# In-projection of a hybrid encoder layer: raw weight blocks fetched one and a half blocks ahead instead of one

## The chip, the cores and the metric

The kernel runs on one core of a Trainium2 chip. Its metric is the device time of one execution in microseconds; lower is better. Instructions are issued on five engines, each of which runs its own stream in order: PE (TensorE), DVE (VectorE), ACT (ScalarE), POOL (GpSimd) and SP (SyncE, which here only issues transfers). ACT issues transfers too, from the same stream as its arithmetic.

## The reference

One layer of a bidirectional encoder, sequence length 1024, model width 1024, float32 in and out. Everything starts with one wide projection whose columns are shared out to three branches and three gates:

```python
xn = rmsnorm(x, norm1_w[l])
p = xn @ w_in[l]
z, xbc, dt_raw, p_rwkv, p_hgrn, p_gate = jnp.split(p, in_splits, axis=-1)
y_ssm  = ssd_branch(z, xbc, dt_raw, ...) @ w_branch_ssm[l]
y_rwkv = rwkv7_branch(p_rwkv, ...)       @ w_branch_rwkv[l]
y_hgrn = hgrn2_branch(p_hgrn, ...)       @ w_branch_hgrn[l]
gates = jax.nn.sigmoid(p_gate).reshape(b, L, N_BRANCH, D_MODEL)
mixed = gates[:, :, 0] * y_ssm + gates[:, :, 1] * y_rwkv + gates[:, :, 2] * y_hgrn
x = x + mixed @ w_out[l]
h_gate, h_up = jnp.split(rmsnorm(x, norm2_w[l]) @ ffn_w_in[l], 2, axis=-1)
x = x + (jax.nn.silu(h_gate) * h_up) @ ffn_w_down[l]
```

The part of the RWKV branch that this document meets often is its preparation: tanh and sigmoid of the low-rank inputs, the decays `exp(-0.6065 * sigmoid(...))`, and the normalised key `kk = k*k_k * rsqrt(sum(...))`, which the kernel computes as an Exp of a Ln.

## The kernel before, in words

**Blocks of the in-projection.** The columns of `w_in` are cut into blocks of 128 (one of 32). One block is a *job* in the class `Jobs`. Job i needs its weights as two fp32r tiles, `wh` (the rounded weights) and `wl` (what the rounding left). `load_w` makes them: a DMA of 512 KB brings the raw block into a tile `wr` (L219, on ACT's queue from the fifth job on), ACT casts it to `wh` (L221), and POOL or DVE subtracts to get `wl` (L223). All three have two buffers. A job then runs 48 matmuls, 24 for each half of the sequence (L330, L331, L332, eight k-tiles of three), and ACT copies each half out of PSUM (L408 or L272).

**When weights are asked for.** `Jobs.steps(i)` is a generator: at its start it calls `load(i + 1)`, so that the raw DMA, the cast and the subtraction of the next block stand one whole block ahead in the order in which the code is written. One step is one k-tile.

**Work between the steps.** The branches call `J.fill(n)` to put n steps between their own instructions, `J.need(job)` to finish a certain job. In the RWKV preparation (`rwkv`, loop over p = 0 to 3, each p a pair of heads) the numbers come from the table `FILL["r1"]`. For p = 0 the written order is: tanh of `wad` (L459), job 2 to its end, sigmoid of its result (L464), sigmoids into `av` (L578) with 3 steps, two rounds of sigmoids into `sg` (L586) and a scan, with 3 steps behind each, then `explog(g)` (L591), then squares, Ln into `kk` (L603), Exp of `kk` (L604), and, in `decays`, Exps into `E` (L622) and `Em` (L623).

**What sets the final order.** The program is built with a scheduler that reorders each engine's stream by a simulated timeline; the written order is a priority, not the result. ACT evaluates functions from sets of tables, of which one is active; ACT_TABLE_LOAD makes another active. Where the scheduler has put the instructions, a later pass walks through ACT's stream and puts a load before each function that the active set lacks. The kernel places one load of its own per p, in `explog`, which activates a set that holds Exp and Ln together:

```python
def explog(g):
    ins = g.nc.scalar.preload_act_table_set("natural_log_exp_and_others")
    g.tc.keep_in_program_order(ins)
```

`keep_in_program_order` pins the load behind the one ACT instruction that was written immediately before it, and behind nothing else. The load has no operands, so the scheduler may put it anywhere after that instruction.

**Further names.** `vx`, `kx`, `rx` are token-shifted projections, `AR` and `BK` the products of `kk`, `rx`, `kx` with the decays, `vps` the transposes of `vx` (PE, L674), `Aps` small Gram products of `AR` and `BK` (PE, L653), `A_sb` their masked copy (DVE, L654), which goes out to DRAM as `As` and comes back as `At` for a triangular inverse on DVE (`lanes`, L483 and L485).

Of the kernel before, what the change touches and what calls it, by code (L numbers as in the profile page):

```python
# [9 lines left out]
F32 = mybir.dt.float32  # L10
# [8 lines left out]
P = 128  # L19
# [3 lines left out]
KT = D // P  # L23
# [25 lines left out]
def f32(ap):  # L49
    return ap.bitcast(F32)  # L50
# [131 lines left out]
class Split:  # L182


    def __init__(self):
        self.hi, self.lo = ([], []), ([], [])
# [25 lines left out]
        x.add(half, hi, lo)  # L212


def load_w(g, src, kt, n=P, tag="w"):

    nc = g.nc
    raw = g.wpool.tile([P, KT, P], F32, tag=tag + "r", name=tag + "r", bufs=g.wraw_bufs)
    g.wq.dma_start(raw[:, :kt, :n], src.rearrange("(k p) c -> p k c", p=P))  # L219
    hi = g.wpool.tile([P, KT, P], F32R, tag=tag + "h", name=tag + "h", bufs=2)  # L220
    nc.scalar.copy(hi[:, :kt, :n], raw[:, :kt, :n])  # L221
    lo = g.wpool.tile([P, KT, P], F32R, tag=tag + "l", name=tag + "l", bufs=2)
    g.lo_eng.tensor_sub(lo[:, :kt, :n], raw[:, :kt, :n], f32(hi[:, :kt, :n]))  # L223
    return hi, lo
# [11 lines left out]
def proj(g, c0, cb, n=P, wsrc=None, x=None, kt=KT):  # L236

    src = (g.A["w_in"][0] if wsrc is None else wsrc)[:, c0:c0 + n]
    whi, wlo = load_w(g, src, kt, n)
    for half in range(2):  # L240
        ps = g.mmps.tile([P, 512], F32, tag="mm", name="mm")
        mm3(g, ps[:n, :], whi, wlo, x or g.x, kt, half, n)
        cb(half, ps[:n, :])


class Jobs:
# [2 lines left out]

    def __init__(self, g):  # L250
        self.g, self.jobs, self.it, self.w = g, [], None, None
        self.started = self.taken = 0

    def add(self, c0, begin, half, end, n=P):
# [22 lines left out]
    def get(self, buf, t):  # L277
        self.need(buf.jobs[t])
        return buf.ap[t]

    def load(self, i):
        g, job = self.g, self.jobs[i]
        g.wq = g.nc.sync if i < 4 else g.nc.scalar
        if i < 4:
            g.lo_eng = g.nc.vector if i < 3 else g.nc.gpsimd
        return load_w(g, g.A["w_in"][0][:, job.c0:job.c0 + job.n], KT, job.n)

    def first(self, half):

# [30 lines left out]
    def steps(self, i):  # L320
        g, job = self.g, self.jobs[i]
        w = self.w or self.load(i)
        self.w = self.load(i + 1) if i + 1 < len(self.jobs) else None
        job.begin()
        n, x = job.n, g.x
        for half in range(2):
            ps = g.mmps.tile([P, 512], F32, tag="mm", name="mm")
            for k in range(KT):
                xh, xl = x.hi[half][k], x.lo[half][k]
                g.nc.tensor.matmul(ps[:n], w[0][:, k, :n], xh, start=(k == 0), stop=False)  # L330
                g.nc.tensor.matmul(ps[:n], w[0][:, k, :n], xl, start=False, stop=False)  # L331
                g.nc.tensor.matmul(ps[:n], w[1][:, k, :n], xh, start=False, stop=(k == KT - 1))  # L332
                if k == KT - 1:
                    job.half(half, ps[:n])
                    if half == 1:
                        job.end()
                        job.done = True
                yield
# [1640 lines left out]
def start(es, tc, A):  # L1979
# [37 lines left out]
    def trans(half):  # L2017
        with tc.tile_pool(name="n1ps", bufs=4, space=PSUM) as pp:
            transpose_split(g, x, half, xs[half * 4:half * 4 + 4], g.vec["norm1_w"], new, pp)

    g.x_load, g.x_rows, g.x_trans = load, rows, trans
    load(0)
    setup_consts(g, tp)
    n1w = vector_rows(g, tp, "n", [[("norm1_w", A["norm1_w"].rearrange("o (k p) -> (o k) p", p=P), 8)]], nc.scalar)
# [111 lines left out]
```

## Time and profile before

| what | value |
|---|---|
| median of 3 runs | 2424.53 us (2424.19 to 2427.28) |
| the profiled execution's own time | 2423.01 us |
| its span in the trace | 2421.3 us |
| mean granted TensorE clock | 0.973 of full speed |
| PE busy | 2272.7 us (94%) |
| DVE busy | 1570.6 us (65%) |
| ACT busy | 988.7 us (41%) |
| POOL busy | 1040.8 us (43%) |
| DMA | 306.23 MB, mean 126 GB/s |
| chain that ended last | PE 61%, DVE 20%, POOL 5%, DMA 5%, issue 4%, ACT 4% |

The busy time is what an engine's own instructions took; its complement is waiting. The chain is followed back from the last instruction: at each step to whatever released it, or to the instruction before it on its engine, so its shares say which engine the time was spent on along the one path that ended last. The profiled execution is 1.5 us (0.06%) under the median of the runs, and 1.7 us of its time lies outside the span.

### The profile page before, as it was taken

How to read it: one execution, taken by the hardware profiler on the slowest of the kernel's cores; microseconds unless marked ns; L12 is line 12 of the kernel's file. 1: busy time of each engine (PE TensorE's matmuls, PEld its weight loads, DVE VectorE, ACT ScalarE, POOL GpSimd, SP SyncE). 2: the span in 40 equal slices, each digit the busy share in tenths (PEclk: the TensorE clock that was granted, in tenths of full speed). 3: DMA queues.
4: the chain of work that ended last, by engine and by line, in shares of the span. 5: the costliest groups of instructions: out<-in, count | busy, mean ns of one | idle time of the engine just before them, and what ended most of it. 6: DMA issues, size and time to landing. Idle time of an engine off the chain costs nothing.

```text
span 2421.3 us, 37438 instructions
## 1 busy us (share of the span) xinstructions
PE 2272.7 (94%) x14785; PEld 1838.1 (76%) x14785; DVE 1570.6 (65%) x2041; ACT 988.7 (41%) x1436; POOL 1040.8 (43%) x817
## 2 busy tenths in 40 slices
PE   8998999999998998998999889999899999999895
PEld 6776778788777877887678567888688888877674
DVE  5678764455558568545856776442764554479999
ACT  6554532222466655435134154332433333344333
POOL 4433331543134335202941841430454444457985
PEclk9999999999999999999999999999999999999998
DMA  5455784764442232245545555541232222244211
GB/s 151 122 139 136 176 212 112 225 199 124 142 150 98 82 118 79 75 160 146 135 156 142 129 191 193 168 130 61 66 101 87 79 87 79 98 163 131 95 54 70
DMA packets 381212, 306.23 MB, mean 126 GB/s; under 512 B 111273, under 2 KB 323149, under 8 KB 381037
## 3 DMA queue, kind: packets, MB, share of 16 engines
q1 hardware_dynamic: 260909, 225.71, 31.7%
q10 hardware_dynamic: 119936, 77.61, 11.1%
q8 instruction: 116, 1.90, 0.3%
q0 software_dynamic: 192, 0.52, 0.1%
q14 instruction: 59, 0.48, 0.1%
HBM read 209.68 MB, written 94.11 MB: 125 GB/s over the span
## 4 chain that ended last, share of the span: by engine, by line
PE 61%; DVE 20%; POOL 5%; DMA 5%; issue 4%; ACT 4%; SPq 1%; ACTq 0%; DVEq 0%; POOLq 0%
PE mm L330 7%; PE mm L331 7%; PE mm L332 7%; PE ps L1588 6%; PE ps L1589 6%; PE ps L1590 6%; DVE ab L1805 3%; DVE acc L1927 2%; PE mm L231 2%; PE mm L232 2%; PE mm L233 2%; DMA E<-cumd 2%; POOL E L1369 2%; DVE rb L1805 1%; PE mm L1588 1%
## 5 line engine op out<-in xcount | busy, mean ns | idle before, releaser
L330 PE MATMUL mm<-x,wh 128*128 128x512 f32 (+1 forms) x1232 | 500.3, 406 | 0.6 <-ACT wh L221 0.5
L331 PE MATMUL mm<-x,wh 128*128 128x512 f32 (+1 forms) x1232 | 492.6, 400 | 0.0
L332 PE MATMUL mm<-x,wl 128*128 128x512 f32 (+1 forms) x1232 | 489.9, 398 | 0.0
L330 PEld LDWEIGHTS mm<-x,wh 128*128 128x128 f32 (+1 forms) x1232 | 232.8, 189 | 62.0 <-issue 10.3
L332 PEld LDWEIGHTS mm<-x,wl 128*128 128x128 f32 (+1 forms) x1232 | 232.8, 189 | 54.2 <-issue 4.6
L331 PEld LDWEIGHTS mm<-x,wh 128*128 128x128 f32 (+1 forms) x1232 | 232.8, 189 | 53.7 <-issue 7.0
L1589 PE MATMUL ps<-xb,rb 128*128 128x512 f32 x432 | 168.3, 390 | 0.0
L1590 PE MATMUL ps<-xb,rb 128*128 128x512 f32 x432 | 168.3, 390 | 0.0
L1588 PE MATMUL ps<-xb,rb 128*128 128x512 f32 x432 | 168.3, 390 | 0.0
L221 ACT CAST wh<-wr 128x1024 fp32r<-128x1024 f32 (+2 forms) x103 | 100.2, 973 | 109.4 <-PE mm L331 87.4
L1588 PE MATMUL ps<-rb,ab 128*128 128x512 f32 x308 | 125.9, 409 | 18.3 <-DVE acc L1927 17.4
L223 POOL TENSOR_TENSOR wl<-wr,wh 128x1024 fp32r<-128x1024 f32 x30 | 79.2, 2640 | 133.9 <-ACT wh L221 109.9
L1589 PE MATMUL ps<-rb,ab 128*128 128x512 f32 x308 | 123.7, 402 | 2.9 <-POOL rb L1805 2.9
L223 DVE TENSOR_TENSOR wl<-wr,wh 128x1024 fp32r<-128x1024 f32 (+2 forms) x73 | 95.2, 1303 | 44.9 <-ACT wh L221 44.8
L1590 PE MATMUL ps<-rb,ab 128*128 128x512 f32 x308 | 122.4, 400 | 1.5 <-DVE ab L1805 1.5
L1752 ACT CAST rb<-fs 128x512 fp32r<-128x512 f32 x85 | 52.6, 622 | 167.2 <-PE ps L1590 117.7
L272 ACT COPY st<-mm 128x512 f32<-128x512 f32 x130 | 75.3, 580 | 99.1 <-PE mm L332 82.9
L1369 POOL TENSOR_TENSOR E<-E,cums 128x1024 f32<-128x1024 f32 x32 | 69.3, 2178 | 65.5 <-DMA E<-cumd 45.3
L810 DVE TENSOR_TENSOR Gc<-Gps,mk 128x256 f32<-128x256 f32 x64 | 27.2, 425 | 106.0 <-PE Gps L807 59.9
L231 PE MATMUL mm<-oh,wh 128*128 128x512 f32 x224 | 89.5, 403 | 6.5 <-DVE gt L1492 4.3
L1927 DVE TENSOR_TENSOR acc<-acc,ps 128x512 f32<-128x512 f32 x148 | 94.1, 674 | 0.0
L1589 PEld LDWEIGHTS ps<-xb,rb 128*128 128x128 f32 x432 | 81.1, 188 | 16.9
(504 smaller groups left out, 5397.2 us busy)
## 6 DMA issues: line engine op xcount, KB each, us to landing
wr<-in_w_in_dram ACTq DMA_DIRECT2D x74, 512.0 KB
fr<-in_ffn_w_in_dram SPq DMA_DIRECT2D x44, 512.0 KB
E<-cumd SPq DMA_DIRECT2D x32, 512.0 KB
pg<-st ACTq DMA_DIRECT2D x48, 256.0 KB
gt<-pg SPq DMA_DIRECT2D x24, 512.0 KB
ad<-a SPq DMA_DIRECT2D x22, 512.0 KB
dr<-in_ffn_w_down_dram SPq DMA_DIRECT2D x22, 512.0 KB
ar<-ad SPq DMA_DIRECT2D x22, 512.0 KB
```

Source lines behind the costliest of these rows:

```text
L221: nc.scalar.copy(hi[:, :kt, :n], raw[:, :kt, :n])
L223: g.lo_eng.tensor_sub(lo[:, :kt, :n], raw[:, :kt, :n], f32(hi[:, :kt, :n]))
L231: nc.tensor.matmul(ps, whi[:, k, :n], xh, start=(k == 0), stop=False)
L330: g.nc.tensor.matmul(ps[:n], w[0][:, k, :n], xh, start=(k == 0), stop=False)
L331: g.nc.tensor.matmul(ps[:n], w[0][:, k, :n], xl, start=False, stop=False)
L332: g.nc.tensor.matmul(ps[:n], w[1][:, k, :n], xh, start=False, stop=(k == KT - 1))
L1369: nc.gpsimd.tensor_tensor(e, e, cs.unsqueeze(2).broadcast_to([P, 8, P]), SUB)
L1588: nc.tensor.matmul(ps, ah, bh, start=(i == 0), stop=False)
L1589: nc.tensor.matmul(ps, ah, bl, start=False, stop=False)
L1590: nc.tensor.matmul(ps, al, bh, start=False, stop=(i == n - 1))
L1805: eng.tensor_sub(blk[:, 1], s, f32(blk[:, 0]))
L1927: nc.vector.tensor_add(m[j], m[j], ps)
```

## The change

`load_w` is split: `load_raw` issues the DMA of the raw block alone, and `load_w` takes a raw tile that is already there. A new method `fetch(i)` calls `load_raw` for job i and keeps the tile; `steps(i)` calls `fetch(i + 2)` at the start of its second half, for jobs from the fifth on. The cast and the subtraction stay where they were. Buffer counts are the same.

```diff
+def load_raw(g, src, kt, n=P, tag="w"):
     raw = g.wpool.tile([P, KT, P], F32, tag=tag + "r", name=tag + "r", bufs=g.wraw_bufs)
     g.wq.dma_start(raw[:, :kt, :n], src.rearrange("(k p) c -> p k c", p=P))
+    return raw
+
+def load_w(g, src, kt, n=P, tag="w", raw=None):
+    nc = g.nc
+    if raw is None:
+        raw = load_raw(g, src, kt, n, tag)
     hi = g.wpool.tile([P, KT, P], F32R, tag=tag + "h", name=tag + "h", bufs=2)
...
+    def source(self, i):
+        job = self.jobs[i]
+        return self.g.A["w_in"][0][:, job.c0:job.c0 + job.n], KT, job.n
+
+    def fetch(self, i):
+        if 4 <= i < len(self.jobs) and i not in self.raws:
+            self.g.wq = self.g.nc.scalar
+            self.raws[i] = load_raw(self.g, *self.source(i))
+
     def load(self, i):
...
-        return load_w(g, g.A["w_in"][0][:, job.c0:job.c0 + job.n], KT, job.n)
+        return load_w(g, *self.source(i), raw=self.raws.pop(i, None))
...
         for half in range(2):
+            if half == 1:
+                self.fetch(i + 2)
             ps = g.mmps.tile([P, 512], F32, tag="mm", name="mm")
```

**What it does to the built program.** On PE, DVE, POOL and SP the instruction streams of the two programs are the same from end to end: the same operations in the same order with the same semaphores, wait values and memory addresses. On ACT all instructions but the table loads are the same and in the same order, the raw DMAs and the casts among them. Only the table loads differ: 52 before, 58 now. Lines shift: L219 is now L217, L221 is L227, L376 is L395, and from L408 on a line of before is 19 lower in the new file (L459 is L478, L603 is L622, L604 is L623, L622 is L641, L623 is L642).

ACT's stream at the tanh of the preparation, before (`av` is the shifted low-rank input, `wr` a raw weight block, `wah` the rounded tanh):

```order
L413 ACTIVATE av<-pt,mu_c_451 128x1024
L219 DMA wr<-in_w_in_dram 128x8x128
L273 DMA ph<-st 128x512
L219 DMA wr<-in_w_in_dram 128x8x128
L459 ACTIVATE av<-av 64x1024
L408 COPY pt<-mm 128x512
L461 CAST wah<-av 128x1024
```

The same place now:

```order
L432 ACTIVATE av<-pt,mu_c_451 128x1024
L217 DMA wr<-in_w_in_dram 128x8x128
L280 DMA ph<-st 128x512
L217 DMA wr<-in_w_in_dram 128x8x128
L395 ACT_TABLE_LOAD
L478 ACT_TABLE_LOAD
L478 ACTIVATE av<-av 64x1024
L427 COPY pt<-mm 128x512
L480 CAST wah<-av 128x1024
```

The second raw DMA, that of the sixth block, stands in the same row of both. `explog`'s load (L395) has come up right behind it, because in the new source this DMA is the ACT instruction written immediately before `explog`; in the old source that was the copy of job 3's first half. The tanh behind it now needs a load of its own.

ACT's stream where `explog`'s load stood before, behind the sigmoids into `sg`:

```order
L464 ACTIVATE sq<-sq 128x1024
L586 ACTIVATE sg<-wps,vcolsv_443 128x512 x2
L408 COPY pt<-mm 128x512
L376 ACT_TABLE_LOAD
L221 CAST wh<-wr 128x1024
L408 COPY pt<-mm 128x512
```

There is none there now, so the sigmoid set stays active until the first Exp. ACT's stream at the Exps and Lns of p = 0, before:

```order
L413 ACTIVATE rx<-pt,mu_c_451 128x1024
L622 ACTIVATE E<-sg 128x8x64 x2
L219 DMA wr<-in_w_in_dram 128x8x128
L603 ACTIVATE kk<-kps,col 128x512
L623 ACTIVATE Em<-sg 128x512
L603 ACTIVATE kk<-kps,col 128x512
L623 ACTIVATE Em<-sg 128x512
L604 ACTIVATE kk<-kk 128x1024
L408 COPY pt<-mm 128x512
```

The same place now (L641 is the Exp into `E`, L622 the Ln into `kk`, L642 the Exp into `Em`, L623 the Exp of `kk`):

```order
L641 ACT_TABLE_LOAD
L641 ACTIVATE E<-sg 128x8x64 x2
L217 DMA wr<-in_w_in_dram 128x8x128
L622 ACT_TABLE_LOAD
L622 ACTIVATE kk<-kps,col 128x512
L642 ACT_TABLE_LOAD
L642 ACTIVATE Em<-sg 128x512
L622 ACT_TABLE_LOAD
L622 ACTIVATE kk<-kps,col 128x512
L642 ACT_TABLE_LOAD
L642 ACTIVATE Em<-sg 128x512
L623 ACTIVATE kk<-kk 128x1024
```

Five loads have come in: the pass has given Exp and Ln sets of their own, and the scheduler's order alternates between the two. For p = 1 to 3 the loads stand as before.

## Rows read from the trace of the kernel before

**Rows 1.** PE's waits, whole run: microseconds in total, times, longest.

```profile
PE Aps L653 <- DVE BK L634: 15.7, 3, 7.8
...
PE yo L1390 <- DVE S L1400: 7.5, 1, 7.5
...
PE vps L674 <- DVE vx L415: 1.7, 1, 1.7
...
PE Rps L824 <- POOL wl L223: 1.1, 1, 1.1
...
PE mm L330 <- ACT wh L221: 0.5, 1, 0.5
```

**Rows 2.** Line L221, what ended idle time before casts; line L219, who waited for it.

```profile
  PE mm L331: 87.4, 32
...
  ACT wh L221: 1.2, 1
```

**Rows 3.** Chain that ended last, 84 to 131 us: start us, us, what.

```profile
89.39 1.06 ACT kk L604
...
106.39 1.21 DVE vx L415
...
107.64 1.09 PE vps L674 x8
...
111.17 0.23 PE mm L330
...
128.76 1.10 PE Aps L653 x32
...
130.61 3.16 DMA As<-A_sb
```

**Rows 4.** Timeline of DVE: start us, us, instruction, [idle before <- releaser].

```profile
90.47 1.29 DVE L605 SCALAR_TENSOR_TENSOR kk<-kx,vcolsv,kk 128x1024 f32<-128x1024 f32 x1 [1.10 <-ACT kk L604]
```

**Rows 5.** Timeline of ACT, 84 to 98 us.

```profile
85.57 1.33 ACT L622 ACTIVATE E<-sg 128x512 f32<-128x512 f32 x2 [0.29 <-PE kps L178]
...
86.90 0.69 ACT L603 ACTIVATE kk<-kps,col 128x512 f32<-128x512 f32 x1
87.48 0.62 ACT L623 ACTIVATE Em<-sg 128x512 f32<-128x512 f32 x1
88.28 0.69 ACT L603 ACTIVATE kk<-kps,col 128x512 f32<-128x512 f32 x1 [0.17 <-PE kps L179]
```

**Rows 6.** Timeline of ACT, 57 to 61 us: a table load between two operations.

```profile
57.42 1.15 ACT L413 ACTIVATE sq<-pt,mu_c 128x1024 f32<-128x1024 f32 x1
58.59 1.28 ACT L578 ACT_TABLE_LOAD   x1
...
59.89 1.27 ACT L578 ACTIVATE av<-aps,vcolsv 128x512 f32<-128x512 f32 x2
```

**Rows 7.** Timeline of ACT at the tanh and behind `explog`'s load.

```profile
49.04 0.39 ACTq L219 DMA_DIRECT2D wr<-in_w_in_dram  x1
51.60 1.06 ACT L459 ACTIVATE av<-av 64x1024 f32<-64x1024 f32 x1 [4.21 <-DVE av L415]
...
71.68 1.05 ACT L221 CAST wh<-wr 128x1024 fp32r<-128x1024 f32 x1 [3.28 <-PE mm L331]
```

**Rows 8.** Stretches behind long waits of PE: us, busy PE, PEld, DVE, ACT, POOL, PEclk, DMA.

```profile
169.38:180.00 10.62, 9.51 (x84) 7.37 (x84) 10.55 (x17) 7.18 (x12) 3.15 (x7) 0.68 0.90 224
239.24:254.00 14.76, 14.76 (x150) 12.06 (x150) 13.13 (x25) 8.71 (x14) 4.33 (x9) 0.59 0.86 206
1149.17:1157.00 7.83, 7.48 (x26) 4.80 (x26) 7.83 (x5) 0.47 (x1) 7.83 (x5) 0.78 0.63 101
```

**Rows 9.** Timeline of PE, 164 to 177 us.

```profile
169.38 1.89 PE L653 MATMUL Aps<-AR,BK 64*64 64x64 f32 x32 [4.78 <-DVE BK L634]
...
174.54 0.63 PE L330 MATMUL mm<-x,wh 128*128 128x512 f32 x1
174.97 0.63 PE L331 MATMUL mm<-x,wh 128*128 128x512 f32 x1
```

More of the change, by code (lines that the diff above doesn't have):

```diff
@@ L212, in transpose_split @@
         x.add(half, hi, lo)
-def load_w(g, src, kt, n=P, tag="w"):
-    nc = g.nc
+def load_raw(g, src, kt, n=P, tag="w"):
     raw = g.wpool.tile([P, KT, P], F32, tag=tag + "r", name=tag + "r", bufs=g.wraw_bufs)
     g.wq.dma_start(raw[:, :kt, :n], src.rearrange("(k p) c -> p k c", p=P))
+    return raw
[3 more added lines that the diff above has]
+        raw = load_raw(g, src, kt, n, tag)
     hi = g.wpool.tile([P, KT, P], F32R, tag=tag + "h", name=tag + "h", bufs=2)
@@ L251, in __init__ @@
         self.g, self.jobs, self.it, self.w = g, [], None, None
+        self.raws = {}
         self.started = self.taken = 0
```

## The prediction

> **What bounds the kernel now.** I read three views in turn. The first is PE's list of waits, because PE is busy 94% of the span and a prefetch can only pay where PE waits for weights. What to see there: of the in-projection's matmuls only one waited for `wh`, 0.5 us, and 1.1 us went to a subtraction `wl` [rows 1]. The long waits are for DVE: 15.7 us in three waits for `BK`, and 1.7 us for `vx` [rows 1]. The second view is the source line of the cast: ACT idled 87.4 us, 32 times, until a matmul (L331) released the `wh` buffer, while the raw DMA's line has one waiter with 1.2 us [rows 2]. The raw block is thus nearly always there before its cast may start, and what a block waits for is the `wh` buffer. The third view is the chain that ended last, between 84 and 131 us, which is where the two programs differ. It runs from the Exp of `kk` on ACT at 89.39 through DVE to `vx` at 106.39, then to `vps` on PE at 107.64, along PE's own matmuls to the Gram product at 128.76, and out by the DMA of `As` at 130.61 [rows 3]. DVE had idled 1.10 us when that Exp released it [rows 4], and PE 1.7 us when `vx` released it [rows 1]. So nothing is left to spare at either handover: a delay of that Exp lands on PE, and on the end.
>
> **The change part by part.**
>
> *The earlier fetch: 0.* In the built program the raw DMAs stand in the same rows as before, with the same waits; the scheduler had already put them there. It adds no DMA, moves none past another on ACT's queue, and SP's and POOL's queues are untouched. Had it moved any, the most it could return is the 0.5 and 1.1 us above.
>
> *One load moved to the tanh, one added there: 0.* The moved load and the new one take 1.28 us each [rows 6], 2.57 together. ACT idles 4.21 us ahead of the tanh; the raw DMA's issue before it ends at 49.43 and the tanh starts at 51.60 [rows 7], which leaves 2.17. The tanh may thus be 0.4 us late. The cast that ACT comes to next but one waits for PE anyway, and PE has no listed wait there [rows 1]. Without that cover it would cost 0.4.
>
> *The load taken away behind the sigmoids: 0.* ACT waits 3.28 us for PE right behind it [rows 7]; the gap only grows.
>
> *Five loads between the Exps and Lns: +6.4.* Here ACT runs through: E, E, kk, Em, kk, Em, kk from 85.57 to 89.39, with only 0.17 us of waiting inside [rows 5]. Each load is 1.28 us, starts 0.02 after the operation before it has ended and lets the next start 0.02 after its own end [rows 6]. Five are 6.4. Two small corrections cancel: neighbouring operations overlap now by some 0.1 (86.90 to 87.48 is 0.58 for an operation of 0.69) and a load ends that, +0.5; and waits inside are swallowed, 0.17 for `kps` and about as much inside the pair of Exps. Stepping through with these durations puts the Exp of `kk` at 95.8 in place of 89.39, and `vps` at 114.0 in place of 107.64. ACT's next operation, a copy out of PSUM, comes 6.4 late too; PE shows no wait for such a copy [rows 1] and comes back to that bank only two halves of a block later.
>
> *TensorE's clock: +3.2.* PE now stands for 1.7 + 6.4 = 8.1 us ahead of `vps`. The 1.7 us wait did not lower the clock. Waits of 4.78, 7.8 and 7.5 us [rows 1, 9] did: in the stretches that follow them the granted clock averages 0.68 over 10.62 us, 0.59 over 14.76 and 0.78 over 7.83 [rows 8]. With the two levels 1.0 and 0.5 (2.4 and 1.2 GHz) that is 6.8, 12.1 and 3.4 us of work at the lower one. A 128x512 matmul is 0.43 us apart there (174.54 to 174.97) [rows 9] and 0.23 otherwise [rows 3], so 47% of such time is lost: 3.2, 5.7 and 1.6 us. I take 3.2: it follows the same sequence (Gram products, `bps`, block matmuls) one pass later. The work behind `vps` is chain up to 128.76 [rows 3], so the loss adds. The ends are 1.6 and 5.7; if the clock held, 0.
>
> *What is late next.* `As` leaves 9.6 us later, so does the triangular inverse on DVE that reads it back, and with it the three waits of PE for `BK` [rows 1]: both sides move together, and the waits stay as long as they are.
>
> **Sum:** 6.4 + 3.2 = +9.6 us. Against the profiled execution, 2423.01, that is 2432.6; the median of the runs is 1.5 above it, so against the median 2424.53 it is **2434.1 us** (+0.4%).
>
> **The rivals.** About 0.2%, 4.9 us, is what a measurement of this kernel can tell from no change.
>
> *A, the forecast:* chance 0.72; by the clock's ends 2432.5 to 2436.6, and with as much again for later stretches at the lower clock that come or go, 2430 to 2439.
>
> *B, the clock holds:* +6.4, 2430.9. For it: the wait of 1.7 us did not lower it. Against it: each of the three long waits, from 4.78 us up, was followed by a stretch at half clock [rows 8, 9]. Chance 0.07.
>
> *C, the delay is taken up (not slower):* the place is the wait of PE for `BK` at 169.38, 4.78 us long [rows 9]. If DVE's inverse there were started by something that does not come behind `vps`, PE could arrive 4.78 us later for nothing, and as much as 7.8 at the second such wait [rows 1]; 9.6 would vanish in the two, and the time be 2424.5. It decides by whether the transfer at 130.61 is what releases DVE; the chain says that it is, and that this transfer comes behind the Gram product at 128.76 [rows 3]. Against it too: all of this lies on the chain of the whole run. A part taken up would leave less than 4.9. Chance 0.12.
>
> *D, a load costs twice its row:* if the operation before a load had to be drained first for as long as the load itself, five would cost 12.8, and with the clock's 3.2 the time would be 2440.5. Against it: the 0.02 us on either side of a load [rows 6]. Chance 0.06.
> The Trainium skill, in "ScalarE: Activation LUTs", section "What ACT_TABLE_LOAD costs", gives 1283 ns for a load and some 1380 ns more for a drain, 2.66 us for every switch. The trace agrees with the first figure (1.28) and shows nothing of the second; by the page the sum would be 13.3 + 3.2 = 16.5 us, an estimate.
>
> *E, the fetch does come earlier and pays:* at most the 0.5 + 1.1 us for weights [rows 1], and the same rows in the streams speak against any of it. 2423 to 2424.5, chance 0.03, of which a third or so for something over 0.2%.
>
> **How the numbers follow.** Slower by over 0.2%: A, B and D, 0.85. Within 0.2%: C and two thirds of E, 0.14. Faster: 0.01. The predicted time is A's. The range runs from 2429.0, under B, to 2439.0, A's upper end: it leaves out C, D and E, 0.21, nearly all of it at the ends.
>
> **What would show it.** In the changed kernel's profile: 58 table loads, with two ahead of the tanh and one each ahead of E, kk, Em, kk, Em at about 85 to 96 us; the Exp of `kk` at about 95.8; PE's wait for `vx` 8.1 us long in place of 1.7; a stretch below full clock behind it that was not there; the transfer of `As` at about 140; and the first wait for `BK` still near 4.8 us, at about 179. If the Exp of `kk` starts by 91 the loads don't cost what their rows say; if the wait for `vx` is 8 us but the wait for `BK` has shrunk, it is C; if all of it holds and the time is still 2424, the delay was given back behind the last of the three waits, and I have misread how PE-bound the rest is.

## The result, and the profile after

| | before | after |
|---|---|---|
| median of 16 runs each | 2424.81 us (2420.36 to 2429.32) | 2433.14 us (2426.08 to 2437.13) |
| ratio, with its 95% interval | | 1.0034 [1.0026, 1.0042] |
| difference | | +8.3 us (+6.3 to +10.2) |
| the profiled execution: time, span, granted clock | 2423.01, 2421.3, 0.973 | 2430.52, 2428.8, 0.971 |

The changed kernel is slower by 0.34%. Of the page, the busy times come first:

```profile
span 2428.8 us, 37444 instructions
...
PE 2275.2 (94%) x14785; PEld 1839.6 (76%) x14785; DVE 1570.2 (65%) x2041; ACT 995.3 (41%) x1442; POOL 1044.0 (43%) x817
```

Every engine but ACT has as many instructions as before; ACT has 1442 in place of 1436, the six table loads more. ACT is busy 6.6 us longer, PE 2.5 us. The span is 7.5 us longer.

ACT's timeline (start us, us, instruction, [idle before <- releaser]) at the tanh and at the Exps and Lns of p = 0, beside [rows 5, 7]:

```profile
49.54 1.28 ACT L395 ACT_TABLE_LOAD   x1 [2.06 <-POOL blk L1003]
50.83 1.28 ACT L478 ACT_TABLE_LOAD   x1
52.12 1.06 ACT L478 ACTIVATE av<-av 64x1024 f32<-64x1024 f32 x1
...
85.64 1.28 ACT L641 ACT_TABLE_LOAD   x1 [0.28 <-PE kps L178]
86.94 1.16 ACT L641 ACTIVATE E<-sg 128x512 f32<-128x512 f32 x2
88.11 1.28 ACT L622 ACT_TABLE_LOAD   x1
89.41 0.69 ACT L622 ACTIVATE kk<-kps,col 128x512 f32<-128x512 f32 x1
90.10 1.28 ACT L642 ACT_TABLE_LOAD   x1
91.40 0.63 ACT L642 ACTIVATE Em<-sg 128x512 f32<-128x512 f32 x1
92.05 1.28 ACT L622 ACT_TABLE_LOAD   x1
93.34 0.69 ACT L622 ACTIVATE kk<-kps,col 128x512 f32<-128x512 f32 x1
94.05 1.28 ACT L642 ACT_TABLE_LOAD   x1
95.34 0.63 ACT L642 ACTIVATE Em<-sg 128x512 f32<-128x512 f32 x1
95.88 1.04 ACT L623 ACTIVATE kk<-kk 128x1024 f32<-128x1024 f32 x1
```

Two loads stand ahead of the tanh, which starts at 52.12 (51.60 before). Five stand among the Exps and Lns, and the Exp of `kk` starts at 95.88 (89.39 before). Each load is 1.28 us with at most 0.03 us on either side.

The handover to DVE, to be read beside [rows 4], and the chain that ended last (start us, us, what), beside [rows 3]:

```profile
96.96 1.28 DVE L624 SCALAR_TENSOR_TENSOR kk<-kx,vcolsv,kk 128x1024 f32<-128x1024 f32 x1 [7.49 <-ACT kk L623]
```

```profile
95.98 0.96 ACT kk L623
...
112.84 1.21 DVE vx L434
...
114.10 1.97 PE vps L693 x8
...
137.25 1.10 PE Aps L672 x32
...
139.09 3.00 DMA As<-A_sb
```

The chain runs over the same stations. `vx` is 6.45 us later, `vps` 6.46, the last Gram product of p = 0 8.49, and the transfer of `As` 8.48. So 6.46 us were lost before `vps` and 2.0 between `vps` and the last Gram product. The `vps` row also shows what happens there: its eight matmuls take 1.97 us in place of 1.09.

PE's waits (us in total, times, longest), beside [rows 1]:

```profile
PE Aps L672 <- DVE BK L653: 15.0, 3, 6.9
...
PE vps L693 <- DVE vx L434: 8.1, 1, 8.1
```

The wait for `vx` is 8.1 us long, 1.7 before. The three waits for `BK` sum to 15.0, 15.7 before, so they have hardly shrunk: DVE and PE are late together. Last, the stretch around `vps` by windows (us, busy PE, PEld, DVE, ACT, POOL, then PE's granted clock, DMA share and GB/s):

```profile
108.00:112.00 4.00, 0.00 (x0) 0.00 (x0) 4.00 (x6) 0.67 (x1) 0.00 (x0) 0.54 0.83 236
112.00:116.00 4.00, 1.90 (x9) 1.57 (x9) 2.04 (x3) 1.85 (x3) 0.36 (x3) 0.50 1.10 274
116.00:120.00 4.00, 4.00 (x41) 3.51 (x41) 1.72 (x3) 3.46 (x7) 2.59 (x4) 0.68 0.60 138
120.00:124.00 4.00, 4.00 (x46) 3.16 (x45) 4.00 (x7) 1.06 (x3) 0.48 (x1) 1.00 0.73 203
```

With the two levels 1.0 and 0.5 (2.4 and 1.2 GHz), a mean of 0.54 over the first 4 us puts the fall at about 108.3, while PE stands, and 0.68 over the third puts the rise at about 118.6. Of these 10.3 us only the 4.5 from `vps` at 114.1 on hold work of PE. In the kernel before, the stretch behind the wait of 1.7 us was at full clock:

```profile
108.00:112.00 4.00, 4.00 (x49) 3.37 (x48) 1.50 (x3) 4.00 (x7) 2.49 (x3) 1.00 0.60 136
```

### The profile page after: what moved, and what is told of

Its sections match the earlier page's. It is cut to its first block, busy times and chain, and to the rows that moved or that the text cites. A ratio compares the mean times of both kernels' runs of the same rounds, so it can differ in the third digit from the quotient of the medians.

```text
span 2428.8 us, 37444 instructions
## 1 busy us (share of the span) xinstructions
PE 2275.2 (94%) x14785; PEld 1839.6 (76%) x14785; DVE 1570.2 (65%) x2041; ACT 995.3 (41%) x1442; POOL 1044.0 (43%) x817
## 4 chain that ended last, share of the span: by engine, by line
PE 59%; DVE 22%; POOL 6%; issue 4%; DMA 4%; ACT 4%; SPq 0%; ACTq 0%; DVEq 0%; POOLq 0%
PE mm L349 7%; PE mm L351 7%; PE mm L350 7%; PE ps L1607 6%; PE ps L1608 6%; PE ps L1609 6%; DVE acc L1946 3%; DVE ab L1824 3%; PE mm L237 2%; PE mm L238 2%; PE mm L239 2%; POOL E L1388 2%; DVE rb L1824 2%; DMA E<-cumd 2%; PE Gps L826 1%
## 5 line engine op out<-in xcount | busy, mean ns | idle before, releaser
L227 ACT CAST wh<-wr 128x1024 fp32r<-128x1024 f32 (+2 forms) x103 | 100.2, 973 | 107.8 <-PE mm L350 77.1
```

## The experiments

The theory was that of the prediction: the fetch does nothing, five loads cost what their rows say, and the half clock behind the longer wait adds to it. Its rivals were that the fetch itself has an effect, that a load costs more than its row, that the path has slack further on, and that the clock is of no account. Each ratio below is against runs of the kernel before on the same chip, made beside it; their medians were 2421.21 us for the first four experiments, 2419.60 for the next four and 2422.02 for the last two.

Executions of the profile start up to 1.8 us apart, so places in time are compared here from one landmark: the start of ACT's shifted `rx` ahead of the Exps (84.13 in the kernel before, 84.21 after). From it on, in us:

| kernel | Exp of `kk` | `vps` | last Gram product, p = 0 | first Gram product that waits for `BK` (its wait) |
|---|---|---|---|---|
| before | 5.26 | 23.51 | 44.56 | 85.25 (4.78) |
| after | 11.67 | 29.89 | 52.97 | 93.40 (4.55) |
| fetch kept, load pinned | 5.26 | 23.52 | 44.57 | 85.01 (4.55) |
| two loads | 7.95 | 26.24 | 50.02 | 90.46 (4.56) |
| ten loads | 18.26 | 36.47 | 59.57 | 100.02 (4.57) |
| clock held | 11.66 | 29.93 | 50.97 | 91.40 (4.56) |
| after, again | 11.66 | 29.88 | 53.47 | 93.90 (4.55) |
| clock held, again | 11.66 | 29.91 | 50.97 | 91.38 (4.51) |

### The fetch without the loads

`explog`'s load is tied to the last ACT instruction that is not a DMA, so that the new DMA in the source no longer draws it forward. The source still fetches early.

```diff
+def behind_last_copy(g, ins):
+    prev = next(i for i in reversed(nc.cur_bb.bb.instructions)
+                if i is not ins.ins and i.engine == ins.ins.engine and i.opcode != "DMACopy")
+    g.tc.add_manual_dep(ins.ins, prev.name, ...)
...
-    g.tc.keep_in_program_order(ins)
+    behind_last_copy(g, ins)
```

> The fetch stays as in the change; only the combined Exp and Ln load is pinned behind the last ACT instruction that is not a DMA. The built streams are then those of the kernel before, 52 loads. If the loads alone made the difference: the Exp of kk at 89.4 us, PE's wait for vx 1.7 us, time as before (ratio 1.000, within 0.1%). If the earlier fetch in the source did something of its own: 2430 us or more (ratio 1.003).

Measured: 2420.10 us, ratio 0.9992 [0.9983, 1.0001]. ACT has 1436 instructions again, and on all five engines the built streams are those of the kernel before. The Exp of `kk`, from ACT's timeline, and `vps`, from PE's, stand as in [rows 3]:

```profile
90.07 1.05 ACT L631 ACTIVATE kk<-kk 128x1024 f32<-128x1024 f32 x1
```

```profile
108.33 1.09 PE L701 MATMUL vps<-ident,vx 128*128 128x128 f32 x8 [1.71 <-DVE vx L442]
```

`vps` waits 1.71 us and takes 1.09, as before. The earlier fetch, as written, does nothing; all of the change's time comes with the table loads. Since this program is the kernel before once more, its trace also shows how far two executions of the same streams lie apart.

### Two loads, and ten

Both take the kernel with the pinned load and put loads into ACT's finished stream right ahead of the Exp of `kk`, alternating between the two sets; nothing else moves. The second has 10 in place of 2.

```diff
+    at = next(k for k, i in enumerate(stream) if i.opcode == "Activation" and i.debug.lineno == 631)
+    for n in range(2):
+        nc.scalar.preload_act_table_set(("exp_and_others", "natural_log_exp_and_others")[n % 2])
+        stream.insert(at + n, nc.cur_bb.bb.instructions.pop())
```

> The streams of the kernel before, with two table loads more right ahead of the Exp of kk. If a load costs its row and the path has no slack: the Exp at 89.4 + 2.6 = 92.0 us, PE's wait for vx 1.7 + 2.6 = 4.3 us, and a run 2.6 us longer if the clock holds, 4.2 to 6 us longer if it falls as it did behind the wait of 4.8 us. If a load had a drain as long as itself: the Exp at 94.5, the wait 6.8. If waits further on take delays up: no longer at all (within 1 us).

Measured: 2425.90 us, 1.0018 [1.0009, 1.0026], which is +4.4 us (2.2 to 6.3); by the time alone the clock's part can't be told from none. The Exp and `vps` come 2.7 us later, the last Gram product 5.46. PE's timeline and the window behind `vps`:

```profile
112.18 1.97 PE L701 MATMUL vps<-ident,vx 128*128 128x128 f32 x8 [4.44 <-DVE vx L442]
```

```profile
112.18:122.00 9.82, 9.82 (x87) 8.13 (x89) 5.45 (x8) 6.63 (x11) 3.58 (x7) 0.69 0.79 207
```

A wait of 4.44 us is followed by half clock: with levels 1.0 and 0.5, a mean of 0.69 over 9.82 us is 6.1 us at the lower one, and at the last Gram product this has cost 2.7. So two loads already bring as large a loss by the clock as after's five, behind a shorter wait.

> The same with ten loads more. If a load costs its row: the Exp at 89.4 + 12.8 = 102.2 us, the wait for vx 14.5 us, 12.8 us longer and 1.6 to 5.7 us for the clock, 2439 to 2443 us. With a drain: the Exp at 115, 2452 us or more. If later waits give up to 5 us back: 2434 to 2438 us.

Measured: 2435.29 us, 1.0057 [1.0044, 1.0071], which is +14.1 us between the medians (10.7 to 17.2 by the interval). The ten loads in ACT's timeline:

```profile
90.40 12.88 ACT L2141 ACT_TABLE_LOAD   x10
```

They take 1.288 us each, with no gap between. The waits of PE in this stretch, 60 to 150 us:

```profile
PE vps L701 <- DVE vx L442: 8.8, 1, 8.8
PE mm L349 <- ACT pt L435: 3.9, 1, 3.9
```

The wait for `vx` was to be 14.5 us long and is 8.8: PE stopped 3.9 us earlier already, because the copy out of PSUM that is queued on ACT behind the loads came late. The delay at `vps` is 12.96 all the same, 15.0 at the last Gram product, and 14.8 at the first wait for `BK`. Ten loads cost ten rows and some clock; the path takes up nothing of it.

### The clock, held through the wait

The changed kernel, with one of its block matmuls repeated 34 times in the wait for `vx`. The copies write what the first one wrote, so PE works on instead of standing.

```diff
+    first = pe[vps - 2]
+    for n in range(34):
+        stream.insert(at + n, first.__replace__(..., sync_info=first.sync_info if n == 0 else None, stop_tensor_calc=True))
```

> The changed kernel with 34 copies of one matmul (the first of the block that is running, same operands, same bank, its result written over with itself) put into PE's stream ahead of the wait for vx, so that PE works through about 7.7 of the 8.1 us. If the lower clock behind that wait is part of the loss: no stretch below full clock before 130 us, the last Gram product of p = 0 at 135.2 instead of 137.25 us, and 2 us less than the changed kernel (2431). If the clock is not on the path: the last Gram product still at 137, 2433 us.

PE's timeline and a window:

```profile
105.94 8.10 PE L349 MATMUL mm<-x,wh 128*128 128x512 f32 x35
114.68 1.09 PE L693 MATMUL vps<-ident,vx 128*128 128x128 f32 x8 [0.42 <-DVE vx L434]
```

```profile
112.00:116.00 4.00, 3.58 (x28) 2.68 (x29) 2.62 (x4) 1.27 (x2) 0.13 (x2) 1.00 1.12 295
```

The clock stays at 1.00, `vps` takes 1.09 us again, and the last Gram product comes 6.41 us later than before in place of 8.41. The 2.0 us behind `vps` are thus the clock's. At the end they don't show: the time is 2429.73 us, 1.0033 [1.0021, 1.0045], +8.5 us. Both kernels were therefore run again on one chip, after:

> The changed kernel once more, beside the next run on the same chip: 8 us above the kernel before.

and held:

> The kernel with the 34 copies of a matmul in the wait for vx once more. If the 2.0 us that the clock returns by the last Gram product of p = 0 reach the end: 2 us below the run of the changed kernel beside it. If later stages give them back: the same as that run.

After: 2430.03 us, 1.0047 [1.0034, 1.0059]. Held: 2428.64 us, 1.0039 [1.0027, 1.0052]. From the landmark, the last Gram product stands at 53.47 after and 50.97 held, so the local gain repeats (2.5 us); the difference of the medians is 1.4 us, and each interval is about 3 us wide on either side. Whether the 2 us reach the end can't be told from this. In DVE's timelines, again from the landmark, the gain lasts to 230 us at least: the product `AR` that starts there in the kernel before comes 6.2 and 6.1 us later with the clock held, 8.2 and 8.7 after. At 263 us the kernel with the pinned load is itself 2.6 us later than the kernel before, with the same streams, so from there on traces of single executions don't tell 2 us apart.

The repeat also shows how much the clock's part differs between executions of one kernel. `vps` waits 8.08 us as before, but more of the half clock behind it holds work:

```profile
115.42:122.00 6.58, 6.58 (x48) 5.59 (x49) 2.21 (x3) 5.98 (x10) 3.11 (x7) 0.57 0.60 135
```

A mean of 0.57 over 6.58 us is 5.7 us at the lower level, 4.5 in the first profile, and the loss by the last Gram product is 2.5 in place of 2.0.

### The raw DMAs later

The prediction held that moving the fetch can return at most what PE waits for weights. The other direction was tried: on the kernel with the pinned load, the first 24 raw DMAs of ACT's queue are issued as late as their blocks allow, right ahead of the next cast or DMA. Each one's waits stay at the old place, so only the transfer moves.

```diff
+    for dma in raw[:24]:
+        at = act.index(dma) + 1
+        while act[at].opcode != "DMACopy" and act[at].debug.lineno != 227:
+            at += 1
+        act.insert(at, dma)
+        act[act.index(dma)] = wait.__replace__(..., sync_info=SyncInfo(on_wait=list(dma.sync_info.on_wait), on_update=[]))
```

> The streams of the kernel before, but the first 24 raw DMAs on ACT's queue (all those up to 420 us) are issued later: not where they stand, but right ahead of the next cast, half a block to a block later; their waits stay at the old place. If a block waits for its buffer and not for its raw weights, there is lead to spare: time as before (within 0.1%), and no cast up to 420 us that waits for its raw DMA. If lead is worth something here: casts that wait for the raw DMA, PE waits for wh, and 5 us or more on the whole.

Measured: 2427.39 us, 1.0036 [1.0023, 1.0048]: slower by about as much as the change. That is the time of the expectation's second case, but of its signs only one is there: one cast waited for a raw block, 5.8 us. PE's wait for `wh` is 0.5 us as in [rows 1], so PE did not wait for late weights of the in-projection. The waits of SP's queue between 100 and 150 us, and DVE's timeline:

```profile
SPq L726 <- DMA wr<-in_w_in_dram: 5.1, 1, 5.1
```

```profile
130.01 0.69 DVE L681 TENSOR_TENSOR A_sb<-Aps,mstrict 128x512 f32<-128x512 f32 x1 [9.34 <-DMA As<-A_sb]
...
143.41 0.19 DVE L510 TENSOR_TENSOR tm<-Wl,At 128x31 f32<-128x31 f32 x1 [9.53 <-DMA At<-As]
```

In the kernel before the last of these is, on the same timeline:

```profile
138.34 0.19 DVE L483 TENSOR_TENSOR tm<-Wl,At 128x31 f32<-128x31 f32 x1 [7.76 <-DMA At<-As]
```

SP's issue of the first `As` write stood until a raw weight transfer of ACT's queue had landed, DVE then waited 9.34 us for that write to free `A_sb`, and the inverse began 5.1 us later (4.8 from the landmark). PE's waits for `BK` grew with it, from 15.7 us (17.8 with the pinned load alone) to 21.5.

Why SP waits for a weight transfer stands in the built program. The DMAs of SP and ACT share eight completion semaphores (`DMAHW0` to `DMAHW7`); each adds 16 to its own when it has landed, and most wait, before they are issued, for the DMA that had the same one before. The seventh raw DMA and the first `As` write follow one another on `DMAHW2` (waits of the instruction just ahead included):

```
ACT L217 DMACopy  wait DMAHW2 >= 128, Pool >= 89   then DMAHW2 += 16
SP  L726 DMACopy  wait DMAHW2 >= 144, DVE >= 94    then DMAHW2 += 16
```

So a raw DMA that is late can hold up what comes next on its semaphore. To see whether that one wait explains the loss, only the DMA that SP waited for, the seventh, was made late (`raw[6:7]` in the diff above):

> The streams of the kernel before with one raw DMA alone issued later, the seventh on ACT's queue (111.7 us before, 120.8 in the run with 24 late ones). If what cost time there was SP's issue of As waiting for this transfer, and not weights that come late: SP waits some 5 us for it again, the triangular inverse on DVE starts at about 143 instead of 138.3 us, no cast waits for a raw DMA, and the run is 3 to 8 us above the kernel before. If the lead of the raw blocks counts: one late block of 24, time as before within 1 us.

```profile
SPq L726 <- DMA wr<-in_w_in_dram: 5.3, 1, 5.3
```

```profile
141.32 0.50 DVE L510 TENSOR_TENSOR tm<-Wl,At 128x31 f32<-128x31 f32 x1 [8.02 <-DMA At<-As]
```

The wait is there and the inverse begins 2.6 us later (3.0, less 0.43 by which this execution's landmark is later). But 2421.71 us, 0.9999 [0.9987, 1.0011]: it costs nothing at the end. The first Gram product that waits for `BK` comes 0.7 us later from the landmark, against 2.9 with all 24, so most of this delay is taken up before PE needs the inverse. A late inverse alone is thus not what a late `vps` is, which holds up PE and DVE together. Then the complement, all but the sixth to eighth (`raw[:5] + raw[8:24]`):

> The same 24 raw DMAs late but for the sixth, seventh and eighth. If the wait of SP at As is the cause and there is lead to spare elsewhere: the inverse starts at 138.3 us as before, and the run is nearer to the kernel before than to the run with all 24 late, by 3 us or more. If lead counts: 21 of 24 blocks are late, so nearly all of that run's 8 us stay.

2424.77 us, 1.0017 [1.0007, 1.0026]. The inverse begins in time (139.61, less 1.51 by the landmark), and SP stands later, for the same kind of transfer, between 150 and 420 us:

```profile
SPq L670 <- DMA wr<-in_w_in_dram: 12.5, 2, 7.6
```

What the longer of them held back stands in the timelines of SP and ACT. SP issues the writes of `BK` and, behind them, `up`, the small weights of the next preparation; ACT's cast of `up` stood 5.92 us, and with it the copies and the `vx` behind it on ACT:

```profile
245.48 8.86 SPq L670 DMA_DIRECT2D BKs<-BK  x2
254.44 0.62 SPq L580 DMA_DIRECT2D up<-in_rwkv_w_up_dram  x1
```

```profile
257.97 0.79 ACT L583 CAST uph<-up 64x256 fp32r<-64x256 f32 x2 [5.92 <-DMA up<-in_rwkv_w_up_dram]
```

With all 24 late the two figures are 8.27 and 6.05 us; with the seventh alone the writes take 1.60 and ACT does not wait there. Across this place, from 245 to 263 us of the kernel before, DVE's delay from the landmark grows from 0.3 to 6.1 us, with all 24 from 3.5 to 8.9. Not all of that is shown to come from `up`, because the kernel with the pinned load is 2.6 us late at 263 us too. In this run two casts also waited for raw blocks, 6.9 us together.

So the 0.36% of all 24 doesn't come from the wait at `As` alone; 0.17% comes with the other DMAs, and for two of them SP's queue waited too, 12.5 us together. How the rest divides stays open: the sixth and the eighth alone were not tried.

### More block work ahead of the waits for BK

A try at a version that beats both: on the kernel with the pinned load, more in-projection steps go ahead of the Gram products of p = 1 to 3, where PE waits for `BK`.

```diff
-            J.fill(F[5])
+            J.fill(F[5] + (0, 7, 11, 4)[p])
```

> The fetch as in the change, the load pinned as in the first run, and more steps of the in-projection written ahead of the Gram products for which PE waits on BK in p = 1 to 3: 7, 11 and 4 steps more. If PE's order of work is what counts and these waits (15.7 us, and some 10 us more by the clock) are room for it: 10 to 20 us below the kernel before, with waits for BK under 5 us in all. If DVE sets the pace of this stage and the steps are only missing further on: no difference, with waits of the same length at other places.

Measured: 2442.36 us, 1.0091 [1.0076, 1.0107], a miss. PE's wait in the list:

```profile
PE Aps L680 <- DVE BK L661: 16.4, 4, 8.0
```

Four waits of 16.4 us replace three of 15.7. The scheduler rewrote the order around the steps, so the block work, to judge by these waits, did not stay in the gap; ACT also has two table loads more (1438 instructions). Where the 22.8 us arise was not followed. No version here beats the kernel before.

## Why the prediction was right

*The fetch, 0:* right. The kernel with the fetch and without the loads is the kernel before, in time and place. That also settles rival E for the program as built. But the sentence beside it, that moving raw DMAs could return at most 0.5 + 1.1 us, was too narrow a bound: it counted PE's waits for weights alone. The late DMAs cost more than that without PE waiting longer for `wh`, part of it, as the traces suggest, through semaphores that they share with SP's DMAs, so a DMA that really moved might change more than the sentence allowed. A fetch that really comes earlier was not tried.

*Two loads at the tanh, 0, and the one removed, 0:* right. The tanh starts 0.5 us later, 0.4 was named. The delay has gone again by the shifted `rx`, which starts 0.08 us apart in the two profiles.

*Five loads, +6.4:* right, to 0.1. The Exp of `kk` is 6.41 us later from the landmark (95.88, forecast 95.8), `vps` starts at 114.10 (forecast 114.0), and the wait for `vx` is 8.1. Each of these five stands behind an ACTIVATE, and ten in a row took 12.88; both refute rival D: nothing is paid beside the row.

*TensorE's clock, +3.2:* the mechanism is right, the size is not; it is 2.0, and 2.5 in the repeat. The term was taken from 6.8 us of half clock behind another wait, and counted all of it as work. In [rows 8] PE is busy 9.51 of that stretch's 10.62 us; the rest is a wait inside the low stretch, in PE's timeline of the kernel before:

```profile
173.10 0.80 PE L179 MATMUL bps<-pl,bd 128*128 128x512 f32 x1 [1.11 <-DVE pl L543]
```

So 5.7 us held work, and the term should have been 2.7. In the changed kernel the lower clock began while PE still stood, at about 108.3, and ended at about 118.6, so of 10.3 us only the 4.5 from `vps` on held work; at 47% that is 2.1 us, and with the repeat's 5.7 it is 2.7. With two loads 6.1 us held work behind a wait of 4.44, and the loss was 2.7. What counts is thus the work in the low stretch and not the length of the wait; why the fall came at different places in the wait stays open. Rival B is refuted for this stretch. The final time alone does not refute it, since 6.4 lies within 6.3 to 10.2, and what the clock's 2 us make at the end stays open.

*What is late next:* right. `As` is 8.48 us late, and the waits for `BK` are 15.0 us against 15.7, so nothing is taken up there, and rival C is refuted: two, five and ten loads arrive at the first wait for `BK` with 5.2, 8.2 and 14.8 us of delay and the same wait of 4.6 us.

*The sum:* 6.46 + 2.0 = 8.5 us by the chain, forecast 9.6, measured 8.3 (6.3 to 10.2). The 1.1 us between forecast and chain are the clock's term. That the end agrees with the chain to 0.2 us is more than one pair of profiles can show, since executions of the same streams differ by more than that further on.

## What to carry to other kernels

Compare the built streams before pricing a change of source: here the rewritten fetch moved no DMA, while a load tied to "the ACT instruction written before it" followed a DMA forward and left the Exps without the table set that they had shared. A table load in a run of ACT work with nothing to spare costs its 1.28 us and, through the wait of TensorE behind it, part of the half clock that follows; count of the low stretch only what holds work. A DMA that is issued later can cost something without TensorE waiting for what it brings, so look in the built program for the DMA that comes next on its completion semaphore, whichever queue issues it.

## What the runs showed that was not expected

- The loss by the clock does not follow the length of the wait: behind a wait of 1.7 us there was none, behind 4.44 us it was 2.7 us at the last Gram product, behind 8.1 us it was 2.0 and 2.5 in two executions, and with ten loads (3.9 and then 8.8 us) again 2.0 (15.0 less 13.0). Two executions of one kernel lie nearly as far apart as the kernels, so no order among them is shown.
- One late raw DMA put the inverse 2.6 us back and cost nothing at the end; 24 put it 4.8 us back and cost 0.36%, while `wh` was never later for PE. That the transfers of raw blocks can cost so much without PE waiting longer for `wh` was not expected.
